# The shared products of an FFN block, moved ahead of its group and summed in PSUM

## The chip, the cores and the metric

The kernel runs on one core of one Trainium2 chip. The metric is the device time of one execution in microseconds (us). A core has TensorE (PE, matrix products), VectorE (DVE), ScalarE (ACT), GpSimd (POOL) and SyncE (SP, which here only issues transfers); each works off its own instruction queue in order and waits for the others on semaphores. Data lie in SBUF; matmul results lie in PSUM, which has eight banks of 128 x 512 float32.

## The reference, cut to what matters

The program is a two-layer encoder on 256 tokens of width 2048. Each layer has a mixer (attention) and then a gated FFN with a short convolution over the tokens; the change touches the FFN's first projection alone:

```python
def conv_ffn(x, w_up, conv_w, conv_b, w_down):
    h = jnp.einsum("bsd,df->bsf", x, w_up)
    g, u = h[..., :D_FF], h[..., D_FF:]          # D_FF = 5632
    gp = jnp.pad(g, ((0, 0), (1, 1), (0, 0)))
    g = conv_w[0] * gp[:, :-2] + conv_w[1] * gp[:, 1:-1] + conv_w[2] * gp[:, 2:] + conv_b
    return jnp.einsum("bsf,fd->bsd", jax.nn.gelu(g) * u, w_down)
```

`x` is the layer's RMS-normalised activation. The kernel multiplies by the row's normalising factor (`rstd`) only after the product.

## The kernel before

**Products in three matmuls.** Every float32 operand is split into a high part (rounded to the format of the matmul) and a low part; a product is high x high + high x low + low x high, three matmuls of 128 x 128 by 128 x 512. The activations are split once (`yT`: 16 tiles of 128 features, each high and low). The weights arrive as they are: one *unit* is 128 x 1024 float32 (two blocks of 128 input features by 512 columns, 512 KB), read by a transfer that SP issues into one of five buffers `raw`; ACT rounds it into `wh` (line 231), DVE subtracts to get `wl` (line 234). `wh` and `wl` are rings of four buffers, so the cast of a unit can start only when PE has finished the unit four places earlier. A unit feeds 12 matmuls: two feature blocks, two halves of the tokens (t = 0, 1), three matmuls each.

**Groups and blocks.** An FFN runs through 11 groups (`up_group`, j = 0 to 10). A group computes 512 columns of the gate branch (x = 0) and 512 of the other branch (x = 1) for all 256 tokens: four PSUM banks, eight units for each x. After groups 0 to 5, and again after 6 to 10, the down projection consumes what the groups made.

**Seven products for eight.** For unit 3 of each group the 2 x 2 blocks (two token halves by two feature blocks, times two feature blocks by two column halves x) are multiplied by seven products instead of eight (`column_forms`, `seven_products`). Three of the seven add straight into a bank of the group. Four (b1, b5, b6, b7) go into four banks of their own (tags `s` and `tp`); each is needed by more than one output. `extra_parts` (lines 841 to 849) combines them on ACT and DVE into four sums in SBUF, `scaled_parts` (line 856) multiplies these by `rstd` on ACT. At a group's end the eviction (line 878, DVE) writes z = bank x rstd + sum for each of its four banks.

**Order within a group before.** Units 0 to 3 are done for x = 0 and x = 1 in turn, then units 4 to 7 for x = 0, eviction, units 4 to 7 for x = 1, eviction. All four banks are of tag `gm`; the next group takes the same four.

**What follows an eviction.** DVE transposes z in 32 x 32 blocks (line 279), and 16 small transfers (line 273; four issued by SP, twelve by POOL) finish the transposition into tile `qk`. Two ticks after the gate branch's eviction `convolved` is recorded: ACT scales (line 896, four instructions, which wait for all 16 transfers), DVE does eight multiply-adds (lines 897 and 899), ACT applies GELU. Two ticks after the other branch's eviction `multiplied` forms the product (line 928) and splits it for the down projection; in three groups of each half it also makes further sums (`row_forms`). A tick is a place in the recording, every 24 matmuls or so. The order of each engine's queue is then settled by a scheduler that goes by its own estimates of durations; on the chip the queue is worked off in that order whatever arrives first.

Of the kernel before, what the change touches and what calls it, by code (L numbers as in the profile page):

```python
# [27 lines left out]
F32 = mybir.dt.float32  # L28
# [5 lines left out]
P = 128  # L34
# [11 lines left out]
UN = 1024  # L46
# [1 line left out]
RAW = 5  # L48
AHEAD = 4
LAST = 2  # L50
UPK = 3
HALVES = ((0, 6, (1, 2, 3)), (6, 11, (1, 2, 3)))


# [17 lines left out]
def trunk_kernel(ctx: ExitStack, tc, a, out):  # L72
# [13 lines left out]
    def nm(s):  # L86
        uid[0] += 1
        return f"{s}_{uid[0]}"
# [5 lines left out]
    def later(delay, fn, rank=2):  # L94

        pending.append((now[0] + delay, rank, fn))
# [19 lines left out]
    def tps(tag, bufs):  # L116
        return psum.tile([P, 512], F32, name=nm(tag), tag=tag, bufs=bufs)
# [179 lines left out]
    def transposes(c, gain, res):  # L297
# [4 lines left out]
        for j in range(4):  # L302
            res[c * 4 + j] = y_tile(ps[j // 2][:, j % 2, :], gain, c * 4 + j)

    def turned_rows(c, gain, res):

        z = att.tile([P, 2, 512], F32, name=nm("z"), tag="sc", bufs=1)
        V.transpose(z, h[:, :, c * 512:(c + 1) * 512])
        pf = att.tile([P, 8, P], F32, name=nm("hT"), tag="pt", bufs=2)
        moved(z.rearrange("p t k -> p (t k)"), pf)  # L310

        def tiles():
            for j in range(4):
                res[c * 4 + j] = y_tile(pf.rearrange("p (t j) q -> p j t q", t=2)[:, j], gain, c * 4 + j)
            if res is formed.get("of") and c == UPK // 2:
                y_forms(pf.rearrange("p (t j) q -> p j t q", t=2), gain)
        return tiles

    formed = {}
# [7 lines left out]
        V.tensor_tensor(f[:, 3], a12, f[:, 1], op=ALU.subtract)  # L327
        return f

    def y_forms(src, gain):  # L330

        y = tmp.tile([P, 2, 2, P], F32, name=nm("yf"), tag="ry")
        for k in range(2):
            S.activation(y[:, k], src[:, UPK % 2 * 2 + k], AF.Copy, scale=gain[:, 2 * UPK + k:2 * UPK + k + 1])
        f = form_sums("scc", *(y[:, k, t] for k in range(2) for t in range(2)))
        form = []
        for x, tag in enumerate(("R", "Rq")):
            high = tmp.tile([P, 2, P], F32R, name=nm("form"), tag="t0")
            low = const.tile([P, 2, P], F32R, name=nm("form"), tag=tag, bufs=1)
            split(high, low, f[:, 2 * x:2 * x + 2])  # L340
            form += [(high[:, k], low[:, k]) for k in range(2)]
        formed["form"] = form

    def row_factor(pin=False, late=False):

# [486 lines left out]
    yT = mixer_out(a["ev_out"], mix, ln[:, 2, :])  # L832


    def up_group(layer, j, yT, rstd, prod, *more):

        sides, extra, sums = {}, [], []
        src = [a["up"][layer, j, x] for x in range(2)]

        def extra_parts():  # L840

            b1, b5, b6, b7 = extra
            s1, x0, x1, y1 = (tmp.tile([P, 512], F32, name=nm("sum"), tag=tag) for tag in ("rx", "ry", "ry", "rx"))
            S.copy(s1, b1)
            V.tensor_tensor(x0, s1, b6, op=ALU.add)
            V.tensor_tensor(x1, x0, b7, op=ALU.add)
            V.tensor_tensor(x0, x0, b5, op=ALU.add)  # L847
# [4 lines left out]
        def scaled_parts():  # L852

            for x in range(2):
                for t in range(2):
                    S.activation(sums[x][t], sums[x][t], AF.Copy, scale=rstd[0][:, t:t + 1])  # L856

        pss = [[tps("gm", 4), tps("gm", 4)] for _ in range(2)]
        for u in range(4):
            if not j and u == 2:  # L860
                rstd.append(row_factor())
            if u == UPK:
                extra += [tps("s", 2), tps("tp", 2), tps("tp", 2), tps("s", 2)]
                seven_products(pss, extra, column_forms(src, u, True), u, yT, formed["form"], True, True)
                later(1, extra_parts)
            else:
                for x in range(2):
                    a_unit(pss[x], src[x], u, yT, KT)
            tick()
        for x in range(2):  # L870
            for u in range(4, 8):
                a_unit(pss[x], src[x], u, yT, KT)
                if u % 2 == 1:
                    tick()
            z = (tmp.tile([P, 8, P], F32, name=nm("z"), tag="z", bufs=1) if x else
                 new_sc().rearrange("p t (f k) -> p (t f) k", k=P))
            for t in range(2):
                out = V.scalar_tensor_tensor(z.rearrange("p (f t) k -> p t f k", t=2)[:, t],
                                       pss[x][t].rearrange("p (f k) -> p f k", k=P), rstd[0][:, t:t + 1],
                                       sums[x][t].rearrange("p (f k) -> p f k", k=P), op0=ALU.mult, op1=ALU.add)  # L880
                if t:
                    tc.keep_in_program_order(out)
# [4 lines left out]
        later(2, lambda: multiplied(j, sides, prod, *more))  # L887

    def convolved(layer, j, sides):

# [123 lines left out]
            tick()  # L1014
        return pss

    def chunk_pair(src, c, act, forms, nk, done):

        nu = nk // 2
        heads = nu - 3 if nu > 10 else nu - 2  # L1020
        pss = pair_head(src, c, act, forms, sorted(forms), heads, nk)
        if not c:
            flush()
        for x in range(2):
            for u in range(heads, nu):
                a_unit(pss[x], src[c + x], u, act, nk)
            if c:
                tick()
            done(pss[x], c + x)

    def ffn(layer, yT, gain, last=False):
        rstd, res = [], None
        for g0, g1, seven in HALVES:
            prod, forms = [], {}
            for j in range(g0, g1):
                up_group(layer, j, yT, rstd, prod, forms, g0, seven)
            nk = 4 * (g1 - g0)
            src = [a["down"][layer, c, 2 * g0:2 * g1] for c in range(4)]
            if g0:
                res = [None] * KT  # L1040
                if last:
                    finish_all(src, prod, forms, nk)
                    return
            for c in (0, 2):
                chunk_pair(src, c, prod, forms, nk, lambda ps, x: finish_chunk(ps, x, gain, res, 1 + x if x < 2 else 1))
        return res

    yT = ffn(0, yT, ln[:, 1, :])
# [280 lines left out]
def _paired_up(w):  # L1329

    w = w.copy()
    x, y = w[:, :, 0, UPK].copy(), w[:, :, 1, UPK].copy()
    w[:, :, 0, UPK] = np.concatenate([x[..., :512], y[..., :512]], axis=-1)
    w[:, :, 1, UPK] = np.concatenate([y[..., 512:], x[..., 512:]], axis=-1)
    return w


# [69 lines left out]
```

## Time and profile before

| | us |
|---|---|
| median of 3 runs (lowest, highest) | 2402.25 (2401.57, 2403.32) |
| the profiled execution, its own time | 2402.49 |
| its span, first to last instruction | 2400.6 |
| PE busy, 10,895 matmuls | 2386.9 |
| DVE busy | 1859.8 |
| ACT busy | 1374.5 |
| POOL busy | 539.7 |

The time of the execution is 1.9 us over its span. TensorE's granted clock is 0.999 of full speed. A matmul's record (390 ns) is longer than its step to the next one, since matmuls overlap; the step is what counts. In the listings an instruction is named by line, engine, operation, and output<-inputs; buffer numbers are left out. "Idle before" is how long its engine did nothing just ahead of it, with what ended that.

### The profile page before, as it was taken

What the parts mean: (1) busy time and instruction counts of PE and PEld (TensorE: products, weight loads), DVE (VectorE), ACT (ScalarE), POOL (GpSimd) and SP (SyncE); (2) the same over time, 40 slices, a digit from 0 to 9 for tenths busy, and PEclk for the clock granted to TensorE, in tenths of its full rate; (3) what the DMA queues carried; (4) which work ended last, traced back from release to release, by engine and by line L of the source; (5) the groups of instructions that cost most, each with busy time, mean ns of one, the idle gap of its engine ahead of it and who ended that gap; (6) DMA issues with size and microseconds to landing.
All of it is one profiled execution on the core that took longest, in us unless ns stands there. A gap on an engine that the chain in (4) does not pass through costs nothing.

```text
span 2400.6 us, 32954 instructions
## 1 busy us (share of the span) xinstructions
PE 2386.9 (99%) x10895; PEld 1983.1 (83%) x10895; DVE 1859.8 (77%) x2461; ACT 1374.5 (57%) x1954; POOL 539.7 (22%) x940
## 2 busy tenths in 40 slices
PE   9999999999999999999999999999999999999998
PEld 7888888888888888888888888888888888888887
DVE  6576567676778898778989867676788887788887
ACT  7455455566556565445656657555565654456664
POOL 1142023322222422004232100422223320033220
PEclk9999999999999999999999999999999999999999
DMA  8778678766767877668777764667678876678874
GB/s 306 208 196 236 198 198 237 211 201 193 215 198 220 222 216 212 204 206 216 213 227 211 220 204 134 188 202 206 208 215 222 217 220 199 207 218 213 241 212 156
DMA packets 287531, 505.64 MB, mean 211 GB/s; under 512 B 159096, under 2 KB 160504, under 8 KB 287360
## 3 DMA queue, kind: packets, MB, share of 16 engines
q1 hardware_dynamic: 256848, 470.15, 64.1%
q0 software_dynamic: 30080, 32.74, 8.0%
q8 instruction: 85, 1.39, 0.2%
q14 instruction: 86, 0.70, 0.1%
q10 hardware_dynamic: 432, 0.66, 0.1%
HBM read 458.48 MB, written 2.18 MB: 192 GB/s over the span
## 4 chain that ended last, share of the span: by engine, by line
PE 59%; DVE 3%; DMA 2%; issue 1%; POOL 1%; ACT 1%; SPq 1%; DVEq 0%; ACTq 0%; POOLq 0%
PE gm L196 16%; PE gm L197 16%; PE gm L195 16%; PE gm L145 2%; DVE wl L234 1%; PE gm L978 1%; PE gm L979 1%; PE gm L977 1%; POOL qk L273 1%; PE gm L150 1%; DMA qk<-z 1%; PE tp L978 1%; PE tp L979 1%; PE tp L977 1%; PE s L978 1%
## 5 line engine op out<-in xcount | busy, mean ns | idle before, releaser
L231 ACT CAST wh<-raw 128x1024 fp32r<-128x1024 f32 (+1 forms) x897 | 936.1, 1048 | 811.5 <-PE gm L197 607.3
L234 DVE TENSOR_TENSOR wl<-raw,wh 128x1024 fp32r<-128x1024 f32 (+1 forms) x897 | 1083.3, 1215 | 383.7 <-ACT wh L231 373.0
L196 PE MATMUL gm<-wl,yT 128*128 128x512 f32 x2092 | 815.6, 390 | 2.3 <-DVE wl L234 2.2
L195 PE MATMUL gm<-wh,yT 128*128 128x512 f32 x2092 | 816.1, 390 | 0.0
L197 PE MATMUL gm<-wh,yT 128*128 128x512 f32 x2092 | 814.6, 389 | 0.0
L196 PEld LDWEIGHTS gm<-wl,yT 128*128 128x128 f32 x2092 | 392.9, 188 | 86.2 <-DVE wl L234 6.3
L197 PEld LDWEIGHTS gm<-wh,yT 128*128 128x128 f32 x2092 | 392.8, 188 | 81.8 <-DVE yT L240 0.2
L195 PEld LDWEIGHTS gm<-wh,yT 128*128 128x128 f32 x2092 | 392.8, 188 | 81.2 <-issue 0.4
L273 POOL DMA_DIRECT2D qk<-sc x264 | 152.2, 584 | 855.3 <-issue 358.4
L273 POOL DMA_DIRECT2D qk<-z x392 | 226.3, 585 | 257.1 <-DVE z L279 232.7
L196 PE MATMUL gm<-wl,prod 128*128 128x512 f32 x518 | 201.5, 389 | 0.0
L195 PE MATMUL gm<-wh,prod 128*128 128x512 f32 x518 | 201.5, 389 | 0.0
L197 PE MATMUL gm<-wh,prod 128*128 128x512 f32 x518 | 201.5, 389 | 0.0
L196 PEld LDWEIGHTS gm<-wl,prod 128*128 128x128 f32 x518 | 97.3, 188 | 20.2
L195 PEld LDWEIGHTS gm<-wh,prod 128*128 128x128 f32 x518 | 97.2, 188 | 20.2
L197 PEld LDWEIGHTS gm<-wh,prod 128*128 128x128 f32 x518 | 97.2, 188 | 20.2
L196 PE MATMUL gm<-wl,mix 128*128 128x512 f32 x256 | 100.1, 391 | 0.4 <-DVE wl L234 0.4
L195 PE MATMUL gm<-wh,mix 128*128 128x512 f32 x256 | 100.0, 391 | 0.0
L197 PE MATMUL gm<-wh,mix 128*128 128x512 f32 x256 | 99.6, 390 | 0.0
L273 POOL DMA_DIRECT2D hT<-z x72 | 41.5, 585 | 199.6 <-PE gm L197 75.4
L856 ACT ACTIVATE sum<-sum,rstd 128x512 f32<-128x512 f32 x88 | 58.9, 716 | 25.4 <-DVE sum L847 16.1
L145 PE MATMUL gm<-yT,wh 128*128 128x512 f32 x256 | 59.5, 390 | 0.0
(356 smaller groups left out, 2640.0 us busy)
## 6 DMA issues: line engine op xcount, KB each, us to landing
raw<-in_up SPq DMA_DIRECT2D x352, 512.0 KB, 4.5
raw<-in_down SPq DMA_DIRECT2D x176, 512.0 KB, 4.4
raw<-in_eva_qk SPq DMA_DIRECT2D x96, 512.0 KB, 4.4
raw<-in_eva_v SPq DMA_DIRECT2D x46, 512.0 KB, 6.0
raw<-in_evb_qk SPq DMA_DIRECT2D x32, 512.0 KB, 4.6
raw<-in_ev_out SPq DMA_DIRECT2D x32, 512.0 KB, 4.3
raw<-in_od_qk SPq DMA_DIRECT2D x32, 512.0 KB, 4.1
raw<-in_od_out SPq DMA_DIRECT2D x32, 512.0 KB, 4.1
```

The costliest lines, as they stand in the source:

```text
L145: T.matmul(ps.rearrange("p a b -> p (a b)"), wh[:, k * P:(k + 1) * P], act[u * 8 + k].rearrange("p a b -> p (a b)"), start=(u == 0 and k = ...
L150: T.matmul(ps[:, 1, :], wl[:, k * P:(k + 1) * P], act[u * 8 + k][:, 0, :], start=False, stop=(u * 8 + k == KT - 1))
L195: T.matmul(ps[t], ah, wh[:, sl], start=(kt == 0), stop=False)
L196: T.matmul(ps[t], ah, wl[:, sl], start=False, stop=False)
L197: T.matmul(ps[t], al, wh[:, sl], start=False, stop=(kt == nk - 1))
L231: first = S.copy(dst_h, src)
L234: V.tensor_tensor(dst_l, src, dst_h.bitcast(F32), op=ALU.subtract)
L273: (nc.sync if i in on_sync else G).dma_start(dst[j * 32:(j + 1) * 32, :, i * 32:(i + 1) * 32], z[i * 32:(i + 1) * 32].rearrange("p (b j c) ...
L856: S.activation(sums[x][t], sums[x][t], AF.Copy, scale=rstd[0][:, t:t + 1])
L977: T.matmul(ps, ah, wh, start=own and first, stop=False)
L978: T.matmul(ps, ah, wl, start=False, stop=False)
L979: T.matmul(ps, al, wh, start=False, stop=own and last)
```

## The change

Group 0 of each layer no longer has the seven products: it runs eight plain units for x = 0 and then eight for x = 1. Each of the groups 1 to 10 has its seven products in two pieces:

- `up_front` records the four shared products (b1, b7, b6, b5; 12 matmuls) within the *previous* group, ahead of its last two units of x = 1. For group 6 that place is in the down projection, ahead of the last two units of its last chunk. The four banks are the ones the running group doesn't use: groups alternate between the four banks `gm` and the four banks `s`, `tp`.
- `merged`, recorded behind the last unit, turns the four banks into the four sums in place: ACT copies b1 out; DVE makes x0 = b1 + b6 and x1 = x0 + b7; DVE writes x0 + b5 into b6's bank and x1 + b5 into b5's bank, ACT copies x1 into b7's bank.
- `up_direct` starts the group with the three products that have one output; it reads the second of the two weight units again, for which there is one transfer more. Then come the seven other units of x = 0 and the seven of x = 1, all added onto the banks.

The eviction is then only z = bank x rstd, on ACT (line 941). Both branches use one tile `z` (a single buffer) for it. The weights of group 0's unit 3 are laid out plainly again.

```diff
-UPK = 3
+UPK = (3,)
...
+    def up_front(layer, j, yT):
+        src = [a["up"][layer, j, x] for x in range(2)]
+        gm = (j >= HALVES[0][1]) == j % 2
+        b1, b7, b6, b5 = (tps(*(("gm", 4) if gm else (tag, 2))) for tag in ("s", "s", "tp", "tp"))
+        direct = []
+        for n, u in enumerate(UPK):
+            w11, t1, t2, t3, t4 = front_forms(src, u)
+            s1, s2, s3, s4 = formed[u]
+            for ps, form, w in ((b1, token_block(yT, 2 * u, 0), w11), (b7, s3, t3), (b6, s2, t2), (b5, s1, t1)):
+                products(ps, form, w, n == 0, u == UPK[-1])
+            direct.append((u, s4, t4))
+
+        def merged():
+            s1, x0, x1 = (tmp.tile([P, 512], F32, name=nm("sum"), tag=tag) for tag in ("rx", "ry", "ry"))
             S.copy(s1, b1)
             V.tensor_tensor(x0, s1, b6, op=ALU.add)
             V.tensor_tensor(x1, x0, b7, op=ALU.add)
-            V.tensor_tensor(x0, x0, b5, op=ALU.add)
-            V.tensor_tensor(y1, x1, b5, op=ALU.add)
-            sums.extend([[s1, x1], [x0, y1]])
-            later(1, scaled_parts)
+            V.tensor_tensor(b6, x0, b5, op=ALU.add)
+            S.copy(b7, x1)
+            V.tensor_tensor(b5, x1, b5, op=ALU.add)
+        return [[b1, b7], [b6, b5]], direct, merged
...
+    def front_forms(src, u):
+        ra, rb = (wts.tile([P, UN], F32, name=nm("raw"), tag="raw", bufs=RAW) for _ in range(2))
...
+        wa, wb = ([wts.tile([P, UN], F32R, name=nm(x), tag=x, bufs=4) for x in ("wh", "wl")] for _ in range(2))
+        split(*wa, ra)
+        V.tensor_tensor(w22, w22, t1, op=ALU.subtract)
+        split(*(x[:, 0:512] for x in wb), w22)
+        split(*(x[:, 512:UN] for x in wb), t1)
...
+    def up_direct(pss, src, yT, u, s4, t4):
+        wh, wl = wunit(src[1][u])
+        products(pss[1][0], s4, [x[:, 0:512] for x in (wh, wl)], onto=True)
+        products(pss[0][0], token_block(yT, 2 * u + 1, 0), [x[:, 512:UN] for x in (wh, wl)], onto=True)
+        products(pss[0][1], token_block(yT, 2 * u + 1, 1), t4, onto=True)
...
+        for x in range(2):
+            for n, u in enumerate(units):
...
+                if x and u == units[-2] and after:
+                    nxt = up_front(*after)
+                if front:
+                    own_unit(pss[x], src[x], u, yT, u == units[-1])
+                else:
                     a_unit(pss[x], src[x], u, yT, KT)
...
+            if nxt:
+                nxt[2]()
+            z = new_z("f k")
             for t in range(2):
-                out = V.scalar_tensor_tensor(...)
+                S.activation(z.rearrange("p (f t) k -> p t f k", t=2)[:, t],
+                             pss[x][t].rearrange("p (f k) -> p f k", k=P), AF.Copy, scale=rstd[0][:, t:t + 1])
```

How the queues stand now, at the end of group 2 of the first layer, is shown at three places; the number behind a name tells tiles apart. First PE, the changed kernel, from the last matmul of the unit ahead of the front (`wh_7163`) to the front's first products (banks `s_7179`, `s_7180`, `tp_7181`, `tp_7182` belong to group 3; `gm` to group 2).

```order
L875 MATMUL gm_6786<-wh_7163,yT_6034 128x512
L875 MATMUL s_7179<-wh_7190,yT_5868 128x512
L875 MATMUL s_7179<-wl_7191,yT_5868 128x512
L875 MATMUL s_7179<-wh_7190,yT_5868 128x512
L875 MATMUL s_7180<-wh_7190,form_5886 128x512
L875 MATMUL s_7180<-wl_7191,form_5886 128x512
```

Behind the 12 matmuls of the front come 12 of the last unit but one (`wh_7220`), 12 of the last unit (`wh_7238`) and then group 3's direct products (`wh_7286`). Second ACT, the changed kernel, over the same stretch: two casts for the front's second buffer, the casts of those three units, and what stands between them; L957 is the first step of the convolution of group 2's gate branch (L896 before).

```order
L231 CAST wh_7192<-raw_7184 128x1024
L231 CAST wh_7192<-t_1302_7187 128x512
L231 CAST wh_7220<-raw_7218 128x1024
L957 ACTIVATE qk_7147<-qk_7057,convb,convw 128x256 x4
L231 CAST wh_7238<-raw_7236 128x1024
L860 COPY sum_7254<-s_7179 128x512
L231 CAST wh_7286<-raw_7284 128x1024
L231 CAST wh_7301<-raw_7299 128x1024
L962 ACTIVATE qk_7147<-qk_7147 128x1024
L231 CAST wh_7319<-raw_7317 128x1024
L941 ACTIVATE z_7263<-gm_6785,rstd_6146 128x4x128
L864 COPY s_7180<-sum_7256 128x512
```

The four L957 stand ahead of the cast of group 2's last unit. Before, at the end of group 2, they stood among the casts of plain units of the next group, with the forms of the seven products behind them:

```order
L231 CAST wh_7370<-raw_7368 128x1024
L896 ACTIVATE qk_7236<-qk_7146,convb,convw 128x256 x4
L231 CAST wh_7388<-raw_7386 128x1024
L231 CAST form_7425<-t_1359_7412 128x512
L231 CAST wh_7415<-raw_7409 128x1024
```

Third DVE, the changed kernel, the same stretch: L958 and L960 are the convolution's eight multiply-adds, L861 to L865 the merging; `wl_7239` is the low part of group 2's last unit, `wl_7287` that of the direct products.

```order
L234 TENSOR_TENSOR wl_7221<-raw_7218,wh_7220 128x1024
L958 SCALAR_TENSOR_TENSOR qk_7147<-qk_7057,convw,qk_7147 128x255
L960 SCALAR_TENSOR_TENSOR qk_7147<-qk_7057,convw,qk_7147 128x255
L958 SCALAR_TENSOR_TENSOR qk_7147<-qk_7057,convw,qk_7147 128x255 x2
L960 SCALAR_TENSOR_TENSOR qk_7147<-qk_7057,convw,qk_7147 128x255 x2
L958 SCALAR_TENSOR_TENSOR qk_7147<-qk_7057,convw,qk_7147 128x255
L234 TENSOR_TENSOR wl_7239<-raw_7236,wh_7238 128x1024
L960 SCALAR_TENSOR_TENSOR qk_7147<-qk_7057,convw,qk_7147 128x255
L861 TENSOR_TENSOR sum_7255<-sum_7254,tp_7181 128x512
L234 TENSOR_TENSOR wl_7287<-raw_7284,wh_7286 128x1024
L862 TENSOR_TENSOR sum_7256<-sum_7255,s_7180 128x512
L863 TENSOR_TENSOR tp_7181<-sum_7255,tp_7182 128x512
```

Seven of the eight multiply-adds now stand ahead of the last unit's low part, and the eighth and the merging ahead of the next group's. The ends of groups 1 to 4 and 6 to 9 of both layers, sixteen in all, read alike on ACT and DVE; the end of group 0 of each layer has the convolution one unit earlier, and ahead of group 6 there is none. Over the whole program PE has 10,901 matmuls (10,895 before), DVE 88 instructions fewer, ACT 34 more, SP 20 transfers more.

More of the change, by code (lines that the diff above doesn't have):

```diff
@@ L870, in up_group, with token_block, products @@
[L870 to L873, printed above, removed]
+            V.tensor_tensor(b6, x0, b5, op=ALU.add)
+            S.copy(b7, x1)
+            V.tensor_tensor(b5, x1, b5, op=ALU.add)
+        return [[b1, b7], [b6, b5]], direct, merged
+    def token_block(act, kt, t):
+        return [act[kt][:, x, t * P:(t + 1) * P] for x in range(2)]
+    def products(ps, form, w, first=False, last=False, onto=False):
+        (ah, al), (wh, wl) = form, w
+        for i, (x, y) in enumerate(((ah, wh), (ah, wl), (al, wh))):
+            T.matmul(ps, x, y, start=first and i == 0, stop=last and i == 2, skip_group_check=onto)
@@ new lines, in up_group @@
+    def up_group(layer, j, yT, rstd, prod, front, after, *more):
+        sides = {}
+        src = [a["up"][layer, j, x] for x in range(2)]
+        if front:
+            pss, direct, _ = front
+            units = [u for u in range(8) if u not in UPK]
+            for u, s4, t4 in direct:
+                up_direct(pss, src, yT, u, s4, t4)
+        else:
+            pss = [[tps("gm", 4), tps("gm", 4)] for _ in range(2)]
+            units = list(range(8))
+        nxt = None
+        for x in range(2):
+            for n, u in enumerate(units):
+                if not j and not x and u == 2:
+                    rstd.append(row_factor())
+                if x and u == units[-2] and after:
+                    nxt = up_front(*after)
+                if front:
+                    own_unit(pss[x], src[x], u, yT, u == units[-1])
+                else:
+                    a_unit(pss[x], src[x], u, yT, KT)
+                if n % 2 == 1 or n == len(units) - 1 and n % 2 == 0:
@@ L1015, in pair_head, with chunk_pair @@
         return pss
-    def chunk_pair(src, c, act, forms, nk, done):
+    def chunk_pair(src, c, act, forms, nk, done, after=None):
         nu = nk // 2
+        nxt = None
         heads = nu - 3 if nu > 10 else nu - 2
@@ L1025, in chunk_pair @@
             for u in range(heads, nu):
+                if x and u == nu - 2 and after:
+                    nxt = up_front(*after)
                 a_unit(pss[x], src[c + x], u, act, nk)
+            if nxt:
+                nxt[2]()
             if c:
@@ L1029, in chunk_pair @@
             done(pss[x], c + x)
+        return nxt
     def ffn(layer, yT, gain, last=False):
-        rstd, res = [], None
+        rstd, res, front = [], None, None
         for g0, g1, seven in HALVES:
@@ L1035, in ffn @@
             for j in range(g0, g1):
-                up_group(layer, j, yT, rstd, prod, forms, g0, seven)
+                front = up_group(layer, j, yT, rstd, prod, front, j + 1 < g1 and (layer, j + 1, yT), forms, g0, seven)
             nk = 4 * (g1 - g0)
```

79 lines of the change are left out of this document (40 added, 39 removed).

## The prediction

> **What bounds the kernel now.** First the page's busy times, then what TensorE waited for:
>
> ```profile
> span 2400.6 us, 32954 instructions
> PE 2386.9 (99%) x10895; PEld 1983.1 (83%) x10895; DVE 1859.8 (77%) x2461; ACT 1374.5 (57%) x1954; POOL 539.7 (22%) x940
> ...
> PE gm L196 <- DVE wl L234: 2.5, 5, 0.9
> PE tp L978 <- DVE wl L234: 0.6, 1, 0.6
> ```
>
> PE is busy through 99% of the span, and none of its waits is for an eviction. Next the groups of the up projection, one window each (busy time of every engine; the sum is over the 18 groups that have one just before them):
>
> ```profile
> 1090.40:1133.30 42.90, 42.90 (x190) 35.48 (x190) 36.20 (x46) 25.45 (x32) 13.84 (x24) 1.00 0.82 222
> 747.10:791.00 43.90, 43.22 (x190) 35.38 (x190) 37.49 (x52) 25.85 (x34) 14.23 (x25) 1.00 0.85 223
> sum 775.70, PE 774.30 PEld 638.27 DVE 667.21 ACT 466.45 POOL 251.93; mean PE 43.02 PEld 35.46 DVE 37.07 ACT 25.91 POOL 14.00
> ```
>
> An undisturbed group takes 42.90 us for its 189 matmuls: 0.227 us a step, 2.72 us a unit. Eighteen at 42.90 are 772.2, so stalls cost these groups 3.5 us in all. Only two things can move the time: the count of matmuls, and stalls of PE. DVE has 37 of 43 us to do, so it recovers slowly, but has slack on average.
>
> How a stall arises is in the second group above. The split of a weight's low part comes 1.2 us too late, behind the product of the branches:
>
> ```profile
> 763.09 1.22 DVE L928 TENSOR_TENSOR qk<-qk,qk 128x1024 f32<-128x1024 f32 x1
> 768.31 2.35 DVE L234 TENSOR_TENSOR wl<-raw,wh 128x1024 fp32r<-128x1024 f32 x2
> 769.58 0.50 PE L196 MATMUL gm<-wl,yT 128*128 128x512 f32 x1 [0.68 <-DVE wl L234]
> ```
>
> That is where the seven products stand: they take three of the four `wh`/`wl` buffers for 21 matmuls, so the ring runs short.
>
> **The change part by part.** Durations, by shape:
>
> ```profile
> L234 DVE TENSOR_TENSOR wl<-raw,wh 128x1024 fp32r<-128x1024 f32 x889 | 1078.0, 1219 | 381.0 <-ACT wh L231 370.3 <-PE gm L150 4.1 <-DMA qk<-z 1.5
> L878 DVE SCALAR_TENSOR_TENSOR z<-gm,rstd,sum 128x512 f32<-128x512 f32 x44 | 30.9, 743 | 0.0
> L845 DVE TENSOR_TENSOR sum<-sum,tp 128x512 f32<-128x512 f32 x22 | 14.9, 679 | 0.0
> L951 DVE TENSOR_TENSOR t<-raw 128x512 f32<-128x512 f32 x45 | 31.0, 689 | 17.2 <-DMA raw<-in_up 10.0 <-DMA raw<-in_down 7.0
> L234 DVE TENSOR_TENSOR form<-sums,form 128x256 fp32r<-128x256 f32 x12 | 4.6, 418 | 0.0
> L324 DVE TENSOR_TENSOR sums<-qk 128x128 f32<-128x128 f32 x12 | 3.4, 284 | 0.0
> L231 ACT CAST wh<-raw 128x1024 fp32r<-128x1024 f32 x889 | 931.4, 1052 | 808.9 <-PE gm L197 607.3 <-DVE raw L955 78.0 <-PE gm L979 21.5
> L856 ACT ACTIVATE sum<-sum,rstd 128x512 f32<-128x512 f32 x88 | 58.9, 716 | 25.4 <-DVE sum L847 16.1 <-DVE sum L845 8.8 <-ACT wh L231 0.2
> L844 ACT COPY sum<-s 128x512 f32<-128x512 f32 x22 | 12.7, 576 | 0.0
> L237 ACT ACTIVATE v<-gm,rstd_par 128x512 fp32r<-128x512 f32 x12 | 8.1, 690 | 2.3 <-PE gm L197 2.3
> ```
>
> *Matmuls.* Group 0 of each layer gets its eighth product back: 2 x 3 x 0.227 = +1.4 us, on the path for certain.
>
> *Evictions and sums.* DVE loses 88 evictions of 0.74 (65 us), ACT loses 88 scalings of 0.72 and gains 88 evictions from PSUM at about 0.69 (the row L237 does just that). The 20 mergings have four adds each, as before, and one copy more. An add or copy whose *output* is in PSUM stands in no row. Between 0.68 (L845, input in PSUM) and 0.74 (L878) for the add, 0.58 (L844) and 0.69 for the copy; I take 0.68 and 0.58, the same form but for the place of the output. None of this is on PE's path by its sum: it is off by about 3 us a group on DVE.
>
> [...]
>
> *Stalls where the seven products stood.* They leave that place: -3.5 us at most; I take all of it, since units in turn leave the ring full.
>
> *The new place.* This carries the sum. In steady state a cast starts when PE releases the buffer and has three units' time:
>
> ```profile
> 736.24 1.40 DVE L878 SCALAR_TENSOR_TENSOR sc<-gm,rstd,sum 128x512 f32<-128x512 f32 x2
> 736.73 1.06 ACT L231 CAST wh<-raw 128x1024 fp32r<-128x1024 f32 x1 [1.67 <-PE gm L197]
> 753.08 1.09 ACT L896 ACTIVATE qk<-qk,convb,convw 128x256 f32<-128x256 f32 x2 [1.74 <-DMA qk<-sc]
> ...
> 1122.47 1.40 DVE L878 SCALAR_TENSOR_TENSOR sc<-gm,rstd,sum 128x512 f32<-128x512 f32 x2
> 1125.72 6.93 POOL L273 DMA_DIRECT2D qk<-sc  x12 [25.44 <-issue]
> 1137.58 2.08 ACT L896 ACTIVATE qk<-qk,convb,convw 128x256 f32<-128x256 f32 x4
> 1138.86 0.87 DVE L897 SCALAR_TENSOR_TENSOR qk<-qk,convw,qk 128x255 f32<-128x255 f32 x2
> 1141.23 0.87 DVE L899 SCALAR_TENSOR_TENSOR qk<-qk,convw,qk 128x255 f32<-128x255 f32 x2
> ...
> ACT qk L896 <- DMA qk<-sc: 12.9, 16, 1.8
> ```
>
> The front takes two of the four buffers for one unit's time of matmuls, so the last unit's cast has two units' time instead of three. Call R the moment at which its buffer is released, 0.2 us after the front's first matmul (records are 0.39 long, steps 0.227). PE wants the low part at R + 5.24 + 0.23 = R + 5.47; cast and split need 1.05 + 1.22 = 2.27. Alone that leaves 3.2 us. But ACT's queue has the convolution's four L957 ahead of that cast, and they wait for the transfers of z.
>
> Let the convolution start at R + d. It started 16.84 us (736.24 to 753.08, having waited 1.74) and 15.11 us (1122.47 to 1137.58, no wait) after its eviction; the 16 waits of 0.8 us on average put the mean at 15.9. The cast at 736.73, released by the end of x = 0, is 0.49 after the eviction's start; R is five units (13.60) later. So d = 16.84 - 0.49 - 13.60 = 2.75, or 1.02, or 1.8 in the mean. The transfers out of tile `z` land sooner than those out of `sc`:
>
> ```profile
> raw<-in_up SPq DMA_DIRECT2D x352, 512.0 KB, 4.5
> ...
> qk<-z POOLq DMA_DIRECT2D x392, 32.0 KB, 3.9
> qk<-sc POOLq DMA_DIRECT2D x264, 32.0 KB, 5.2
> ```
>
> By 1.3 us: d from -0.3 to 2.75, mean 0.5 (as z) to 1.8 (as sc). All moves now go out of `z`, so I take 0.9, nearer to that row.
>
> Then ACT is done with the convolution at d + 2.08 and with the cast at d + 3.13. DVE's multiply-adds step by 0.4 (eight from 1138.86, the last two at 1141.23); seven stand ahead of the split, which starts at d + 3.4 and ends at d + 4.62: late by d - 0.85. Behind it on DVE: the eighth multiply-add, x0, the direct products' split, x1, and only then the add into b6's bank, with which the next group begins: 1.13 + 0.4 + 0.6 + 1.13 + 0.6 after the split's start, 0.68 long, so done at d + 7.94. PE, already delayed by d - 0.85, wants it at d + 7.1 to d + 7.3: late by another 0.7. Together about d - 0.15 for each such end of a group, if d exceeds 0.15. At d = 0.9 that is 0.75.
>
> In ten of the sixteen ends (groups 2 to 4 and 8, 9 of both layers) `row_forms` of the group before lies on DVE ahead of the transposition of z: four sums at 0.28 and two splits at 0.42, 2.0 us, of which the wait for the second eviction covers half; d grows by 1.0. So 6 x 0.75 + 10 x 1.75 = 22.0 us. Bounds: d = -0.3 gives 10 x 0.55 = 5.5, d = 2.75 gives 6 x 2.6 + 10 x 3.6 = 51.6, d = 1.8 gives 36.4. The ends of group 0 have a unit more of time and the convolution a unit earlier in the queue: within half a microsecond each, in the range.
>
> *Transfers.* Twenty reads of 512 KB more, at 4.5 us to landing behind five buffers; DMA was busy 0.76 to 0.85 of the time in these groups. I cost them at nothing: the ring of five `raw` buffers hides them, and SP's z transfers stand where DVE's transposition is due anyway. Without that cover, see the third rival.
>
> *Sum.* From the profiled execution, 2402.49 (0.24 above the median of the runs): + 1.4 - 3.5 + 22.0 = 2422.4, so **2422 us**.
>
> **The rivals.** What a measurement here can tell from no change is about 0.2%, 2397.7 to 2407.3.
>
> *The ring covers it: not slower.* If the last transfer lands at d below 0.15, also where sums lie ahead, the last unit's split is in time and the eighth multiply-add no longer matters; then 2402.5 + 1.4 - 3.5 + 0 to 5.5 = 2400 to 2406. For it: 3.9 us for z; DVE has 65 us less to do. Against it: the convolution started no sooner than 15.0 us after an eviction in the two rows above, and waited in sixteen of 22 groups. [...]
>
> *Faster by over 0.2%.* It needs 5 us. Stalls in the groups are 3.5 in all and the matmuls cost 1.4 back: 2400.4 is the floor unless the matmul's step falls.
>
> *The weight ring starves.* The front holds two `raw` buffers from landing to their last split, the third read follows at once. If one transfer (4.5 us) were half uncovered at each of the 20 fronts, 20 x 2.25 = 45 us come on top of the first sum without the convolution's: 2445, or 2467 with it. Against it: a read lands within two units' time.
>
> **How the numbers follow.** Late convolution 0.65 (own range 2409 to 2440), the ring covers it 0.22, starving weights 0.09, faster 0.04. Same takes in the second and little of the first: faster 0.04, same 0.23, slower 0.73. The range, 2402 to 2440, reaches down through the second case and leaves out the third and the upper bound d = 2.75.
>
> **What would show it.** Right: PE waits for DVE's `wl` once, and for the add L863 once, at each of sixteen ends; L957 idle ahead of it on ACT, ended by the transfers of z; windows of groups with sums longer than those without; no stall elsewhere in the groups. Wrong: groups of 42.9 us throughout (the ring covers it), or waits of L880's users for `raw` (starving). What would break the working is the landing: it was taken from another place in the program, beside other reads.

## The result and the profile after

| | before | after |
|---|---|---|
| median (lowest to highest), us | 2401.91 (2399.75 to 2403.32) | 2470.15 (2469.01 to 2478.71) |
| ratio, 95% interval | | 1.0293 (1.0268 to 1.0317) |
| span of the profiled execution, us | 2400.6 | 2467.9 |

The change costs 68 us, 2.9%. The prediction said 2422 with a range to 2440: the right side, and a third of the size. The page of the changed kernel:

```profile
span 2467.9 us, 33119 instructions
PE 2411.8 (98%) x10901; PEld 1990.3 (81%) x10901; DVE 1792.7 (73%) x2373; ACT 1373.4 (56%) x1988; POOL 538.6 (22%) x940
```

DVE has 67 us less to do (65 were worked out), PE six matmuls more. No engine has become the bound; PE waits. Its waits (us in total, times, longest) and the wait of the convolution on ACT:

```profile
PE gm L875 <- DVE wl L234: 9.1, 8, 1.2
PE tp L875 <- DVE wl L234: 8.8, 8, 1.2
PE gm L196 <- DVE wl L234: 8.7, 7, 2.4
PE gm L875 <- ACT wh L231: 5.1, 5, 1.7
PE tp L875 <- ACT wh L231: 5.0, 4, 2.8
PE gm L875 <- DVE gm L863: 2.8, 6, 0.7
...
PE tp L875 <- DVE tp L863: 1.2, 3, 0.6
...
ACT qk L957 <- DMA qk<-z: 70.7, 18, 5.7
```

L875 are the products of a group. Of their waits the prediction named two: the one for DVE's half of a weight (`wl`), sixteen times, once at each end of a group, and the one for the add into b6's bank (L863), nine times. Nine waits for ACT's half (`wh`) stand beside them. How much they cost a group is seen between the first matmuls of two successive fronts, 189 matmuls apart. Fourteen such stretches lie in the up groups. Of thirteen of them (the first, 44.19 us from 698.69, is left out) two and the sum are shown (length, then busy time of PE, PEld, DVE, ACT, POOL, then PE's granted clock and the DMA share):

```profile
742.88:792.09 49.21, 45.13 (x190) 36.55 (x189) 35.22 (x48) 26.35 (x36) 13.79 (x24) 0.97 0.76 214
...
1147.53:1192.95 45.42, 43.55 (x191) 35.32 (x189) 35.04 (x48) 26.14 (x36) 13.80 (x24) 1.00 0.73 209
...
sum 598.79, PE 573.31 PEld 464.09 DVE 452.31 ACT 340.48 POOL 179.21; mean PE 44.10 PEld 35.70 DVE 34.79 ACT 26.19 POOL 13.79
```

598.79 / 13 = 46.1 us where an undisturbed group took 42.90. One end of a group in time order, group 6 of the second layer:

```profile
2160.12 0.39 PE L875 MATMUL gm<-wh,yT 128*128 128x512 f32 x1
...
2162.47 2.08 ACT L957 ACTIVATE qk<-qk,convb,convw 128x256 f32<-128x256 f32 x4 [3.78 <-DMA qk<-z]
...
2164.46 1.04 ACT L231 CAST wh<-raw 128x1024 fp32r<-128x1024 f32 x1
...
2166.01 1.22 DVE L234 TENSOR_TENSOR wl<-raw,wh 128x1024 fp32r<-128x1024 f32 x1
...
2167.28 0.50 PE L875 MATMUL tp<-wl,yT 128*128 128x512 f32 x1 [1.22 <-DVE wl L234]
...
2169.86 0.69 DVE L863 TENSOR_TENSOR gm<-sum,gm 128x512 f32<-128x512 f32 x1
...
2170.70 0.47 PE L875 MATMUL gm<-wh,form 128*128 128x512 f32 x1 [0.63 <-DVE gm L863]
```

The front starts at 2160.12, so R = 2160.35. The convolution, for which ACT has been idle for 3.78 us until z's transfers landed, starts at R + 2.12; ACT's cast of the last unit and DVE's split stand behind it in order, and PE waits for the split and then for the add.

For all ends together: d is the start of the convolution less R, and the loss of an end is the time from the front's first matmul to the 90th after it, less 90 steps of 0.2267 us (an undisturbed end gives 0.14 by that reckoning). Over the sixteen ends of the prediction d is 2.83 us in the mean (1.39 to 5.24) and the loss 3.49 (1.57 to 6.37), 55.8 in all.

### The profile page after: what moved, and what is told of

Read it like the earlier page. It is cut to its first block, busy times and chain, and to the rows that moved or that the text cites. A ratio compares the mean times of both kernels' runs of the same rounds, so it can differ in the third digit from the quotient of the medians.

```text
span 2467.9 us, 33119 instructions
## 1 busy us (share of the span) xinstructions
PE 2411.8 (98%) x10901; PEld 1990.3 (81%) x10901; DVE 1792.7 (73%) x2373; ACT 1373.4 (56%) x1988; POOL 538.6 (22%) x940
## 3 DMA queue, kind: packets, MB, share of 16 engines
q8 instruction: 85, 1.39, 0.2%
## 4 chain that ended last, share of the span: by engine, by line
PE 59%; DMA 16%; DVE 13%; POOL 4%; issue 4%; ACT 2%; SPq 1%; DVEq 0%; ACTq 0%; POOLq 0%
PE gm L196 14%; PE gm L195 14%; PE gm L197 14%; DMA qk<-z 11%; POOL qk L273 4%; DVE wl L234 4%; PE s L875 4%; PE gm L875 3%; DMA raw<-in_up 3%; PE gm L145 2%; DVE qk L958 2%; DMA raw<-in_down 1%; DVE z L279 1%; DVE qk L960 1%; SPq L273 1%
## 5 line engine op out<-in xcount | busy, mean ns | idle before, releaser
L273 POOL DMA_DIRECT2D qk<-z x656 | 377.5, 583 | 1160.8 <-DVE z L279 967.7
L196 PE MATMUL gm<-wl,yT 128*128 128x512 f32 x988 | 385.4, 390 | 2.2 <-DVE wl L234 2.2
L195 PE MATMUL gm<-wh,yT 128*128 128x512 f32 x988 | 386.8, 392 | 0.4 <-ACT wh L231 0.4
L197 PE MATMUL gm<-wh,yT 128*128 128x512 f32 x988 | 385.2, 390 | 0.0
L875 PE MATMUL gm<-wh,yT 128*128 128x512 f32 x928 | 298.5, 397 | 5.1 <-ACT wh L231 5.1
L875 PE MATMUL s<-wh,yT 128*128 128x512 f32 x720 | 228.0, 390 | 0.0
L875 PE MATMUL tp<-wh,yT 128*128 128x512 f32 x672 | 214.2, 394 | 5.1 <-ACT wh L231 5.0
L196 PEld LDWEIGHTS gm<-wl,yT 128*128 128x128 f32 x988 | 185.7, 188 | 40.4 <-DVE wl L234 3.3
L197 PEld LDWEIGHTS gm<-wh,yT 128*128 128x128 f32 x988 | 185.5, 188 | 39.1 <-DVE yT L240 0.2
L195 PEld LDWEIGHTS gm<-wh,yT 128*128 128x128 f32 x988 | 185.6, 188 | 38.5 <-ACT wh L231 0.9
L875 PEld LDWEIGHTS gm<-wh,yT 128*128 128x128 f32 x928 | 177.6, 191 | 45.2 <-ACT wh L231 7.7
L196 PE MATMUL gm<-wl,prod 128*128 128x512 f32 x518 | 202.1, 390 | 6.2 <-DVE wl L234 6.2
L875 PE MATMUL gm<-wl,yT 128*128 128x512 f32 x464 | 184.9, 398 | 9.1 <-DVE wl L234 9.1
L875 PEld LDWEIGHTS s<-wh,yT 128*128 128x128 f32 x720 | 135.3, 188 | 28.6
L875 PEld LDWEIGHTS tp<-wh,yT 128*128 128x128 f32 x672 | 127.3, 190 | 33.9 <-ACT wh L231 7.4
L875 PE MATMUL tp<-wl,yT 128*128 128x512 f32 x336 | 132.9, 395 | 8.8 <-DVE wl L234 8.8
L875 PE MATMUL s<-wl,yT 128*128 128x512 f32 x360 | 140.3, 390 | 0.0
L196 PEld LDWEIGHTS gm<-wl,prod 128*128 128x128 f32 x518 | 97.2, 188 | 27.7 <-DVE wl L234 7.5
```

Of the source, the lines that this page charges most:

```text
L195: T.matmul(ps[t], ah, wh[:, sl], start=(kt == 0), stop=False)
L196: T.matmul(ps[t], ah, wl[:, sl], start=False, stop=False)
L197: T.matmul(ps[t], al, wh[:, sl], start=False, stop=(kt == nk - 1))
L273: (nc.sync if i in on_sync else G).dma_start(dst[j * 32:(j + 1) * 32, :, i * 32:(i + 1) * 32], z[i * 32:(i + 1) * 32].rearrange("p (b j c) ...
L875: T.matmul(ps, x, y, start=first and i == 0, stop=last and i == 2, skip_group_check=onto)
```

## The experiments

Each is told against two theories and sometimes a third: the late convolution (theory 1), and a front that starves the rings of weights wherever the convolution stands (rival 2). "Kept in order" in the edits below is the helper `tc.keep_in_program_order`, which holds an instruction at its place in the recording; recorded at `later(3)` and kept in order, the four scalings of the convolution stand on ACT where the changed kernel has them, ahead of the cast of the last unit. The scheduler orders the rest anew. In second_moves_8_8 and reads_held all sixteen ends read on ACT and DVE as in the changed kernel, up to the transposition of the second z; in conv_no_wait, moves_8_8 and all_moves_8_8 all eight multiply-adds (not seven) stand ahead of the last unit's split, and the transposition of the second z stands one split later.

**The convolution out of the way.**

```diff
-                later(2, lambda: convolved(layer, j, sides))
+                later(5 if after else 2, lambda: convolved(layer, j, sides))
...
-            S.activation(c, g, AF.Identity, ...)
+            tc.keep_in_program_order(S.activation(c, g, AF.Identity, ...))
```

> Edit: the convolution of a group's gate branch is recorded at the first tick of the next group and kept in that order, so that on ACT its four scalings stand behind the casts of the last unit and of the next group's first two units, and behind the copy of b1. Theory 1 (its wait for z's transfers holds up the last unit's cast): the 59.5 us that the 18 fronts within up groups lost go, 2470 - 59.5 = 2411 us (2406 to 2418). Rival 2 (the front itself starves the rings of weights, wherever the convolution stands): the stalls stay, 2450 or more. Rival 3 (not the wait but the convolution's work, 2.1 us on ACT and 3.4 on DVE, is too much at a group's end): 2411 too, since the work has moved as well.

2414.72 us; ratio to before 1.0052 (1.0037 to 1.0067). Every one of the 18 ends loses 0.14. PE's longest waits are now these, and no line of L875 is among them:

```profile
PE gm L196 <- DVE wl L234: 5.9, 7, 1.6
PE s L1040 <- DVE wl L234: 3.4, 2, 1.8
```

Rival 2 is out as the cause of the loss: the front stands where it stood. What is left stands at the starts of the down projections.

**The same place, the same work, no wait.**

```diff
...
+                sides['z'] = z
...
-            g, c = g4[:, i, :], c4[:, i, :]
+            g, c = sides['z'][:, 2 * i:2 * i + 2, :].rearrange("p a b -> p (a b)"), c4[:, i, :]
...
```

The convolution reads z before the transfers have put it in order, so this kernel leaves out their part of the transposition.

> Edit: the convolution stands in ACT's and DVE's queues where it stands in the changed kernel, between the casts of the last two units, with all its instructions, but reads z as it lies right after the 32 x 32 transposition, which is done some 12 us sooner than the transfers; what it computes is therefore not the convolution. Theory 1: no wait, so cast and split are in time (split done at R + 3.5, wanted at R + 5.47), 2408 to 2418. Rival 2: 2450 or more. Rival 3: the work still stands there, 2440 or more.

2411.68 us; 1.0038 (1.0023 to 1.0052); 0.14 at every end. So it is the wait that costs, not the 2.1 us of ACT and 3.4 of DVE, all of which stand here ahead of the last unit's cast and split.

**The transfers shared otherwise.** The third argument says which of four groups of four transfers SP issues: `(3,)` is four, `(1, 3)` eight.

```diff
-            turned(z..., sides[x]..., (3,))
+            turned(z..., sides[x]..., (3,) if x else (1, 3))
```

> Edit: of the 16 transfers of the gate branch's z SP issues eight and POOL eight (before: four and twelve); the convolution's place in the queues is as in the changed kernel. Theory 1: POOL's issue takes 4.4 us for 6.6, SP's 5.4 for 2.7, so z lands 1.2 to 2.2 us sooner; d falls from 2.83 to 0.6 to 1.6, the loss at the 16 ends from 3.49 to about d + 0.4 = 1.0 to 2.0 each, 2470 - 24 to 40 = 2430 to 2446. Rival 2: SP's reads of weights stand behind four transfers more, so 2470 or more.

2412.48 us; 1.0043 (1.0028 to 1.0058): better than theory 1 said, and the other way from rival 2. The last transfer landed 8.7 us after the start of the transposition, not 14.35, which is 5.7 us sooner where 1.2 to 2.2 were worked out from the issue times. Of the listing of DMA issues (KB each, median us to landing), the changed kernel and this one:

```profile
qk<-z POOLq DMA_DIRECT2D x656, 32.0 KB, 4.5
...
qk<-z SPq DMA_DIRECT2D x304, 32.0 KB, 2.7
```

```profile
qk<-z POOLq DMA_DIRECT2D x568, 32.0 KB, 3.0
...
qk<-z SPq DMA_DIRECT2D x392, 32.0 KB, 2.4
```

POOL's transfers themselves land sooner. Why is taken up by the last experiment. Fifteen of the sixteen ends lose 0.14.

**The convolution directly behind the last cast.** As the first edit, with `later(4 if after else 2, ...)`.

> Edit: the convolution is recorded behind the last unit and kept in that order: on ACT directly behind that unit's cast, but still ahead of the copy of b1 and of the next group's casts. Theory 1: the last unit is in time; the chain x0, split, x1, b6 add now ends about 6.9 us after the convolution's start where 7.9 after R is wanted: late by d - 1.0 = 1.8 and a few tenths for the restart, 16 x 2.1 = 34 for 55.8, 2448 (2435 to 2455). So it must lie between conv_late and the changed kernel. Rival 2: 2470.

2484.99 us; 1.0349 (1.0334 to 1.0365): slower than the changed kernel, so this expectation failed. The last unit is in time, but the loss at the ends is 4.31. The end of group 1 of the second layer:

```profile
1816.12 2.08 ACT L957 ACTIVATE qk<-qk,convb,convw 128x256 f32<-128x256 f32 x4 [1.73 <-DMA qk<-z]
...
1821.90 0.50 PE L875 MATMUL gm<-wl,yT 128*128 128x512 f32 x1 [0.16 <-DVE wl L234]
...
1823.10 0.50 PE L875 MATMUL gm<-wh,form 128*128 128x512 f32 x1 [0.47 <-DVE gm L863]
...
1824.18 1.25 DVE L279 STREAM_TRANSPOSE z<-z 128x1024 f32<-128x1024 f32 x1 [0.54 <-ACT z L941]
...
1825.35 4.59 DVE L234 TENSOR_TENSOR wl<-raw,wh 128x1024 fp32r<-128x1024 f32 x4
...
1826.59 0.50 PE L875 MATMUL gm<-wl,yT 128*128 128x512 f32 x1 [1.37 <-DVE wl L234]
```

The expectation counted the first two waits. It left out a third: in this kernel's queue the transposition of the other z stands directly behind the merging on DVE, one split earlier than in the changed kernel. It waits for ACT's eviction, the next unit's split waits behind it, and PE waits about 1.4 us again (at eleven of the sixteen ends). And d has grown to 4.01; the transposition of the gate branch's z, at 3.47 us after the last matmul, is later than in the changed kernel (2.35).

**How lateness is handed on.** The end of group 8 of the first layer in the changed kernel shows that. PE's last matmul for the gate branch starts at 1179.12:

```profile
1175.84 1.23 DVE L989 TENSOR_TENSOR qk<-qk,qk 128x1024 f32<-128x1024 f32 x1 [2.15 <-DMA qk<-z]
...
1179.39 1.43 DVE L234 TENSOR_TENSOR prod<-qk,prod 128x256 fp32r<-128x256 f32 x4
...
1180.02 1.26 ACT L941 ACTIVATE z<-s,rstd 128x512 f32<-128x512 f32 x2
...
1182.80 1.24 DVE L279 STREAM_TRANSPOSE z<-z 128x1024 f32<-128x1024 f32 x1
```

The product of the branches of group 7 (L989) waits for the second z's transfers. Its casts and splits stand ahead of group 8's eviction on ACT and transposition on DVE, which starts 3.68 us after the last matmul. Before, eviction and transposition were both DVE's, the transposition right behind the eviction, 1.42 us after the last matmul at every end. In the kernel before, at group 1 of the first layer:

```profile
736.24 1.40 DVE L878 SCALAR_TENSOR_TENSOR sc<-gm,rstd,sum 128x512 f32<-128x512 f32 x2
737.67 1.25 DVE L279 STREAM_TRANSPOSE sc<-sc 128x1024 f32<-128x1024 f32 x1
```

The experiment on this:

```diff
-            turned(z..., sides[x]..., (3,))
+            turned(z..., sides[x]..., (1, 3) if x else (3,))
```

> Edit: only the other branch's z goes by eight transfers of SP and eight of POOL; the gate branch's, for which the convolution waits, keeps four and twelve. On DVE the product of the branches and its splits stand three weight splits earlier than in the changed kernel, since the order is made for the earlier landing. Theory (lateness is handed on: the second z lands late, the product of the branches and its splits are late on DVE, and with them the next gate branch's eviction and transposition): the transposition starts 1.15 after the last matmul at nearly every end instead of 2.35 in the mean, so d = 1.15 + 14.35 - 14.06 = 1.4 for 2.83; the loss at an end is about d + 0.3 = 1.7, 16 x 1.7 = 28 for 55.8, and some 6 us at the starts of the down projections go too: 2470 - 28 - 6 = 2436 (2428 to 2446). Rival (d is set by the gate branch's own transfers alone): only the 6 us go, 2464.

2431.08 us; 1.0115 (1.0099 to 1.0130). The transposition starts at 1.21 in the mean, d is 1.45 (1.4 expected), the loss 1.89 (1.7). So of the mean d of 2.83, about 1.4 goes with the second z (lateness handed on by the group before) and 1.4 stays with the gate branch's own transfers. The edit changes two things about the second z, though: it lands earlier, and its product stands earlier in DVE's queue; they were not told apart. The wait of the convolution is still there:

```profile
ACT qk L957 <- DMA qk<-z: 64.6, 21, 4.5
```

**Both, and what is left then.** All z go by eight and eight (in this program leaving the third argument out does the same; the convolution is recorded at `later(3)` and kept in order):

```diff
-            turned(z..., sides[x]..., (3,))
+            turned(z..., sides[x]..., (1, 3))
```

> Edit: as moves_8_8, and the other branch's z too goes by eight transfers of SP and eight of POOL. The late convolution is gone already (2412.5); what is left over before is 10.1 us, of which 1.2 are the six matmuls (1.4) and the rest stands at the starts of the down projections, whose last group of products waits for that other z. Theory (the landing of the second z behind POOL's twelve transfers): it lands 4 us sooner there too, 2404 to 2408. Rival (those stalls come of the eviction on ACT, or of the order on DVE): 2412.

2403.24 us; 1.0005 (0.9996 to 1.0014), no difference from before. The stretches of 189 matmuls in this kernel:

```profile
742.33:785.31 42.98, 42.98 (x190) 35.48 (x189) 35.22 (x49) 26.42 (x38) 9.20 (x16) 1.00 0.80 232
...
sum 558.83, PE 558.83 PEld 461.17 DVE 450.49 ACT 339.88 POOL 119.55; mean PE 42.99 PEld 35.47 DVE 34.65 ACT 26.14 POOL 9.20
```

558.83 / 13 = 42.99 us, PE busy throughout, 40 us less than the changed kernel's thirteen. Here the place of the front costs nothing.

With the convolution at `later(5 if after else 2, ...)` on top of that:

> Edit: all_moves_8_8 and conv_late together. If all_moves_8_8 has no wait left at the ends of groups (0.14 each), taking the convolution out of the way as well changes nothing: 2403 within 2 us. Below 2400 would mean that the convolution still cost something; above 2406, that its later place hurts the products of the last group of a half.

2403.99 us; 1.0006 (0.9998 to 1.0015). The two cures do not add up: there was one loss.

The same edit of the transfers in the kernel before:

> Edit: the kernel before, with the 16 transfers of both z shared eight and eight. The z lands 4 us sooner there as well. If its convolution's wait cost PE nothing in that kernel (nothing urgent stands behind it on ACT), the time stays: 2402 within 2 us.

2402.97 us; 1.0003 (0.9994 to 1.0012). The last transfer of the gate branch's z lands 8.6 us after the start of the transposition here, for 14.22. The kernel before has nothing to gain from that; only the new place of the front made the landing matter.

**How near the third rival was.**

The edit is made to all_moves_8_8:

```diff
-RAW = 5
+RAW = 4
```

> Edit: as all_moves_8_8 with four buffers for the incoming weights instead of five. The prediction costed the 20 transfers more at nothing because five buffers hide them; its third rival was that the front starves them. If five are ample, one less costs 0 to 3 us. If the front is near starving them, one less costs half a transfer (2.25 us) at each of the 20 fronts, 45 us.

2441.66 us; 1.0164 (1.0150 to 1.0178), 38 us more than all_moves_8_8. ACT's wait for incoming weights, 5.3 us in three waits in all_moves_8_8 with five buffers, is with four:

```profile
ACT wh L231 <- DMA raw<-in_up: 127.9, 92, 4.6
```

With five the front's 20 transfers more cost nothing that all_moves_8_8 shows, as taken; but the ring has not one buffer to spare. Of the 36.3 us by which this profiled execution is longer, 23 lie in the up groups and 13 in the down projections and mixers. The kernel before was not run with four buffers, so how much of this is the front's stays open.

And on top of raw_4, two units of a group by seven products, where the changed kernel has one (the front's work for one unit now stands in `piece`, called as `nxt[3]`):

```diff
-UPK = (3,)
+UPK = (3, 5)
...
-                if x and u == units[-2] and after:
+                if x and u == units[-5] and after:
...
+                    nxt[3](0)
+                if x and u == units[-2] and after:
+                    nxt[3](1)
```

> Edit: raw_4 with a second unit (5) by seven products in groups 1 to 10: its four shared products go onto the same four banks, so the merging is paid once; unit 3's front stands ahead of the fifth unit from the end, unit 5's ahead of the last but one, and the second pair of split fourth forms has a tile of its own (the 4 KB for which raw gave up a buffer). 20 groups x 3 matmuls x 0.227 = 13.6 us less for PE; DVE has about 4.8 us more to do in each group, 39 of 42. If the late convolution was all that was wrong with the place, this gains: raw_4's time less 8 to 14 us, 2391 to 2400. If two buffers more per group or DVE's load bind, raw_4's time or more.

2541.07 us; 1.0585 (1.0570 to 1.0599). This was the attempt at a kernel that beats both, and it loses 139 us, 99 beyond raw_4: PE now waits above all for casts, ACT waits for reads, and so does DVE with the fronts' first sums (`t`). Which of the rings is short was not tried.

```profile
PE s L877 <- ACT wh L231: 26.3, 14, 4.1
...
ACT wh L231 <- DMA raw<-in_up: 80.0, 68, 8.3
DVE t L886 <- DMA raw<-in_up: 72.4, 21, 6.4
```

**Why POOL's transfers land late.** SP's queue in the changed kernel, at a transposition of the gate branch's z that starts at 1090.16 (POOL issues its twelve from 1091.69 to 1098.6):

```profile
1088.72 0.33 SPq L128 DMA_DIRECT2D raw<-in_up  x1
1091.42 2.55 SPq L273 DMA_DIRECT2D qk<-z  x4
1094.08 7.82 SPq L128 DMA_DIRECT2D raw<-in_up  x5
```

While SP waits for the transposition its reads of weights are held back; then five are issued within 7.8 us. POOL's transfers issued before the first of them landed within 2.6 us, those issued from 0.2 us ahead of it and later took 3.9 to 7.2. Over the sixteen ends the median is 2.3 us for the 68 issued earlier and 6.2 us for the 124 issued later. In moves_8_8 127 of POOL's 128 are issued earlier. The experiment lets SP issue something useless first:

```diff
+                for k in range(8):
+                    nc.sync.dma_start(fill[k], z...[96:128, 8 * k:8 * k + 8])
                 later(3 if after else 2, lambda: convolved(layer, j, sides))
```

> Edit: the moves of z stay four and twelve, the convolution stays where it stands in the changed kernel; behind its four transfers of the gate branch's z SP issues eight tiny ones (32 x 8 elements into scratch that nobody reads), so that its next read of weights is issued some 5 us later. Theory (POOL's later transfers land late because SP's next 512 KB read is issued ahead of them; those issued before it land in 2 to 3 us, those behind it in 4.6 to 6.6): POOL's twelve are all issued before that read, the last lands about 7.8 + 2.3 = 10.1 after the transposition's start instead of 14.3, and d is negative as in moves_8_8: 2408 to 2418. Rival (twelve in POOL's own queue are slow by themselves): landing and time stay, 2470; or more, since weights are read later.

2430.21 us; 1.0115 (1.0098 to 1.0132): the direction of the theory, but 40 us where it gave 52 to 62. POOL still issues twelve in 6.9 us, but in one such stretch (the end of group 6 of the second layer) they now land in 2.4 us in the median, against 5.3 in the changed kernel. First the changed kernel, then this one:

```profile
qk<-z POOLq DMA_DIRECT2D x12, 32.0 KB, 5.3
```

```profile
qk<-z POOLq DMA_DIRECT2D x12, 32.0 KB, 2.4
```

What was mis-sized: eight tiny issues took 3.84 us and not 5, so that POOL's last transfers still met the reads (16 of 192 over the sixteen ends, 4.3 us in the median), and the lateness handed on by the other z (transposition at 2.63) is untouched. The last landing is 12.05 us after the transposition's start; d is 0.84, the loss 1.42.

```profile
1082.48 2.55 SPq L273 DMA_DIRECT2D qk<-z  x4
1085.08 3.84 SPq L949 DMA_DIRECT2D fill<-z  x8
1089.03 1.79 SPq L128 DMA_DIRECT2D raw<-in_up  x4
```

All runs on one scale, in us: means over the sixteen ends, worked out from the starts of the instructions and the landings of the transfers in each trace.

| run | transposition after the last matmul | landing after that | d | loss of an end | median |
|---|---|---|---|---|---|
| before | 1.42 | 14.22 | | | 2402 |
| changed kernel | 2.35 | 14.35 | 2.83 | 3.49 | 2470.15 |
| conv_behind_cast | 3.47 | 14.47 | 4.01 | 4.31 | 2484.99 |
| second_moves_8_8 | 1.21 | 14.08 | 1.45 | 1.89 | 2431.08 |
| reads_held | 2.63 | 12.05 | 0.84 | 1.42 | 2430.21 |
| moves_8_8 | 3.21 | 8.69 | -1.28 | 0.30 | 2412.48 |
| all_moves_8_8 | 1.22 | 8.31 | -1.75 | 0.14 | 2403.24 |
| conv_no_wait | 3.17 | 14.50 | -1.75 | 0.14 | 2411.68 |
| conv_late | 2.43 | 14.45 | not ahead of the cast | 0.14 | 2414.72 |

Where z lands in time, d is -1.75 because ACT then comes to the convolution right behind the cast ahead of it.

## Why the prediction was wrong in size, step by step

**Right.** PE bounds (busy for 98% of the span). DVE's relief brought nothing: all_moves_8_8, which has it and no stall at the ends, is no faster than before. The six matmuls' 1.4 us fit that run too, though its interval is too wide to show them. The old stalls behind the seven products are gone (in all_moves_8_8 PE is busy through all of the thirteen stretches, 558.83 us). The new loss is PE waiting, because the convolution's wait stands ahead of the last cast; conv_late and conv_no_wait show this directly. The wait for `wl` came at each of the sixteen ends as forecast, the wait for L863 at nine; in the other seven PE ran at about half its clock just then (a step of 0.427 us for 0.227) and came later than the add. The unknown adds and copies into PSUM were sized well: L863 takes 0.69 us (0.68 taken) and L864 0.58 (0.58 taken). With its output in PSUM the add is 0.01 us longer than that of the row (0.69 for 0.68, L845).

**Mis-sized: d.** This is the step that failed: the time at which z has landed and the convolution can start. The prediction took d = 0.9 us, plus 1.0 in ten ends: 1.5 in the mean. Measured 2.83, which is 16 x 1.3 = 21 us.

- "All moves now go out of `z`, so I take 0.9": the two rows for tiles `z` and `sc` were read as a property of the tile. But the landing out of `z` came 14.35 us after the transposition, where out of `sc` it was 14.22 before: the rows told of the place in the program, and reads_held shows what in that place matters: the reads of weights that are issued beside the transfers (issued later, the landing comes at 12.05). Without the credit the step has d = 1.8, its own value for `sc`.
- The step kept the 1.4 us from eviction to transposition. The diff drops the line that tied the transposition to the eviction and puts the eviction on another engine; from then on each waits in a queue of its own, behind the late product of the group before (2.35 us after the last matmul for 1.42, +0.9).
- "Where sums lie ahead d grows by 1.0": not seen. d is 2.79 in the ten ends with sums and 2.91 in the six without.

**Mis-sized: the loss for a given d.** The prediction had d - 0.15; measured, less the 0.14 of an undisturbed end, d + 0.52, which is 16 x 0.67 = 11 us. The waits themselves came out as worked out: in the end shown, the split starts 3.54 after the convolution (3.4 taken). In seven of the sixteen ends PE ran at about half its clock behind the waits (a step of 0.427 us), and these lose d + 1.0 as against d + 0.15 in the other nine (the 0.14 taken off). The rest is that the step behind a wait is about 0.1 us longer as well (0.31 to 0.34 us for 0.227, where the lower clock has not set in).

**Left out.** The ends of group 0, "within half a microsecond each": 1.35 and 2.30, 3.4 us beyond the undisturbed. And the starts of the four down projections, which the prediction did not look at. One such start in the changed kernel:

```profile
949.72 0.69 DVE L1012 TENSOR_TENSOR t<-raw 128x512 f32<-128x512 f32 x1 [3.31 <-DMA raw<-in_down]
...
951.46 1.22 DVE L989 TENSOR_TENSOR qk<-qk,qk 128x1024 f32<-128x1024 f32 x1
...
955.82 3.49 DVE L234 TENSOR_TENSOR wl<-raw,wh 128x1024 fp32r<-128x1024 f32 x3
...
957.09 0.50 PE L196 MATMUL gm<-wl,prod 128*128 128x512 f32 x1 [1.34 <-DVE wl L234]
```

The product of the last group's branches (L989) and its splits push those of the weights back. What DVE waits for ahead of the product is, at all four starts, a read of the down projection's weights (2.6 to 3.8 us); the second z has landed 0.4 to 1.7 us before the product starts. In all_moves_8_8 these stalls are nearly gone (PE's waits for `wl` at L196 are 0.2 us in all, 8.7 in the changed kernel); whether by the earlier landing of z or by the order of the queues made for it is not shown. The waits of over 0.2 us at the starts of the changed kernel come to some 11 us more than before. Together, from the profiled execution of before: 2402.5 + 1.4 - 3.5 + 53.6 (sixteen ends) + 3.4 + 11 = 2468.4, against the profiled execution's 2469.6 (2467.9 and the 1.7 around it).

**The rivals.** "The ring covers it", 2400 to 2406, is what all_moves_8_8 is: a condition on the landing, which the changed kernel misses by 2.7 us. "The weight ring starves", 2445 to 2467, gave the nearer number for the wrong reason. The direction held because a convolution that is late can only cost PE time, and just 3.5 us of gain stood against it. The upper bound of d, 2.75, was left out of the range on the strength of the one row that pointed the other way, and it was nearly the true mean. Even with it the prediction's sum gives 2402.5 + 1.4 - 3.5 + 51.6 = 2452; the loss for a given d and the starts of the down projections make up the rest. One reading beside the sum was off as well: the old stall shown at 769.58 is 0.68 us, not 1.2.

## What to carry to other kernels

When an edit moves a step between a transfer and its user, take the time until the user's data land from rows at that place, with the reads that will be issued beside them; a median of another tile's transfers is no property of the tile (here 14.35 us out of `z` and 14.22 out of `sc`, where the medians before were 3.9 and 5.2). An instruction that waits for a transfer belongs behind everything urgent in its engine's queue, or its transfers must be ahead of the bulk reads: either cure alone brought back 55 to 58 of 68 us here. Directly behind the last cast was not far enough (conv_behind_cast, 2484.99 us). And where an eviction moves to another engine, what followed it without a wait now follows two queues (the transposition here: 2.35 us after the last matmul for 1.42), so ask what is late in either.

## What the runs showed of the hardware that was not expected

**About half the clock behind some waits.** Behind the waits at the end of group 1 of the first layer (length, busy times, and the granted clock as the last but two):

```profile
751.00:753.00 2.00, 0.49 (x1) 0.19 (x1) 2.00 (x4) 2.00 (x4) 0.00 (x0) 1.00 0.00 0
753.00:757.00 4.00, 3.85 (x10) 3.04 (x11) 4.00 (x8) 3.69 (x5) 0.00 (x0) 0.57 0.59 142
757.00:766.00 9.00, 9.00 (x41) 7.41 (x40) 7.00 (x7) 4.49 (x5) 6.18 (x11) 1.00 0.79 203
```

There the matmuls' step is 0.427 us, then 0.227 again. The groups' ends of the changed kernel have seven such stretches, of five to eight steps each; from 846.20 to 849.00, within one of them, the granted clock is 0.50. The two waits ahead of them, with one matmul between, come to 1.95 to 4.51 us together. Another end with 2.9 us of waits (group 8 of the first layer) has none. In all_moves_8_8 there is none in the groups. That the stretches follow waits is seen; what decides was not tried.

**Small transfers behind a bulk read.** At the end of group 6 of the second layer POOL's 32 KB transfers took 5.3 us in the median in the changed kernel, where SP issued reads of 512 KB in the midst of them, and 2.4 in reads_held, where it issued these later. They were slowed, not held until the reads were done: in the stretch at 1090.16 the first that was issued beside the reads landed at 1097.89, the first of the reads at 1099.45.
